# A hybrid attention block: softmax rows left unnormalised, inverse sums carried through DRAM into the gate factor, and three orders changed

## The chip, the core and the metric

The kernel runs on one core of one Trainium2 chip. The metric is the device time of one execution in microseconds (us); three runs of the kernel before had a median of 450.83 us (450.81 to 453.52). The engines are TensorE (PE in the profile; PEld is its loading of weights), VectorE (DVE), ScalarE (ACT), GpSimd (POOL) and SyncE (SP), each with one queue of instructions that it works off in order.

## What is computed

The input x is 512 x 1024 float32. A root-mean-square norm and one wide projection give, for two attention branches of 8 heads of 64 each, q, k, v and a gate input z, and for the merge two gate inputs ga and gb. Cut to what matters here:

```
h = rms_norm(x, norm_g);  proj = h @ w_in          # fq fk fv fz mq mk mv mz ga gb fl
p = softmax(logits, axis=-1);  y = p @ v           # per head; fox: forget bias, moba: rope, causal
y_fox  = from_heads(fox_attention(...))  * silu(fz)
y_moba = from_heads(moba_attention(...)) * silu(mz)
merged = sigmoid(ga + b0) * (y_fox @ w_fox) + sigmoid(gb + b1) * (y_moba @ w_moba)
out = x + merged @ w_out
```

Each row of p is exp(logit - max) over its sum. The row of p is a query's, so the same number divides the whole output row of that query and head; the gate factor silu(z) multiplies that output row element by element.

## The kernel before

**Precision.** Products are float32 made of three matmuls: each operand is split into a rounded part (hi, written by ACT) and the rest (lo, by DVE), and hi*hi, hi*lo and lo*hi are summed in PSUM. `split` (L107) does it for weights: ACT copies (L110), and DVE subtracts (L112). With its argument `half` set, DVE subtracts the first two of four parts (128x512) and POOL the last two, both on L112; without it DVE subtracts all (128x1024). `HALF[0]`, which stands for that argument for projection weights of q, k, v and z, is set at the start of attention.

**Stages.** The program has four. "start" projects the first q and k of the fox branch, norms x, then computes the z units fza and fzb (L372 to L374; the gate factor silu(z) is kept in ZS), the forget bias (`forget`, DVE lines L422 to L447) and the v units fva; between those `make_sums` (L227) builds sums and differences of the normed input's blocks (DVE L236, L240) and stores them in DRAM (POOL L242), for the gates' products. "attention" runs four groups of four heads each: fox a, fox b, moba a, moba b. "gates" computes ga and gb by a scheme of seven products instead of eight for each pair of 256 columns (units GA0, GA1, GB0, GB1; PE L664 to L667; `finish` adds the bias and the sigmoid, L674), reading the sums back (`load_sums`, POOL L249). "end" is the projection by w_moba's rest and w_out.

**One group of attention** (`attn_group`) has pairs of heads. Tr (L475, L477) transposes q and k of a pair; ACT and DVE write QS, KH, KL (L484 to L489). Aa(h) makes a head's logits in four row blocks of 128, 256, 384 and 512 columns (lg, L511, L512); DVE adds the mask and finds the maximum (L514), ACT takes the exponential and, with it, the row sums rs (L516), DVE inverts the sums (L520) and scales the rows of p (L522):

```
if i % 2:
    V.reciprocal(ri[:, hh, i - 1:i + 1], rs[:, hh, i - 1:i + 1])
    for n in range(i - 1, i + 1):
        V.tensor_scalar(pts[n], pts[n], ri[:, hh, n:n + 1], None, op0=OP.mult)
```

Bb(h) transposes p into p_a, p_b and p_cc (L533), splits them (pth by ACT L538, ptl by DVE L539) and multiplies by v (pv, L542, L543); the result, feature by query, is put into ypair by ACT (ysh, L567) and DVE (L568). Yp multiplies the pair's ypair by the gate factor (L577) and splits it (yhf, ylf and so on, L578, L579). The norm of q and k (`ss`, `ff`, L295 to L303) runs on DVE and POOL.

**Order.** The lists `order` and `plan` give for each group the projection units ("filler") that are woven between its pieces by `inter`; `pump` loads and splits their weights a few units ahead, in `order`'s sequence. A tile scheduler then orders the instructions of each engine by its own estimate of time, so that the program's text isn't the final order. Tiles come from pools with a fixed number of buffers by tag.

Of the kernel before, what the change touches and what calls it, by code (L numbers as in the profile page):

```python
# [29 lines left out]
def fox_moba_kernel(ctx: ExitStack, tc, xT, x, w_in, w_fl, w_fox, w_moba, w_out, cst, rope, out):  # L30
# [18 lines left out]
    def t2(tag, bufs, name, shape=(P, 512), dt=F32):  # L49
        pool = stage["pool"] if tag in ("qs", "pt", "ys") else sb  # L50
        return pool.tile(list(shape), dt, name=name, tag=tag, bufs=bufs)
# [176 lines left out]
    def make_sums(k):  # L228
        def tl(tag, dt=F32):
            return stage["pool"].tile([P, 512], dt, name=f"sum_{tag}", tag=tag, bufs=2)  # L230
        a, b = XT[k], XT[k + 4]
        f0, f1 = tl("sf"), tl("sf")
        s3, s2, s1, s4 = f0[:, 0:HT], f0[:, HT:S], f1[:, 0:HT], f1[:, HT:S]
        for o, x, y, op in ((s3, a[:, 0:HT], a[:, HT:S], OP.subtract), (s1, a[:, HT:S], b[:, HT:S], OP.add),
                            (s2, s1, a[:, 0:HT], OP.subtract), (s4, b[:, 0:HT], s2, OP.subtract)):
            V.tensor_tensor(out=o, in0=x, in1=y, op=op)  # L236
        for i, f in enumerate((f0, f1)):
            hl = [tl("sh", F32R), tl("sl", F32R)]
            A.activation(hl[0], f, AF.Copy)
            V.tensor_tensor(out=hl[1], in0=f, in1=hl[0].bitcast(F32), op=OP.subtract)  # L240
            for d, t in zip(S_dram, hl):
                nc.gpsimd.dma_start(out=d[2 * i:2 * i + 2, :, k, :].rearrange("s p t -> p s t"),  # L242
                                    in_=t.bitcast(F32).rearrange("p (s t) -> p s t", t=HT))
# [155 lines left out]
    def zero_kl():  # L399
        for o in range(2):  # L400
            KLt[o] = [stage["pool"].tile([P, S], F32R, name=f"KL{o}{b}") for b in range(2)]
            Q2t[o] = stage["pool"].tile([P, S], F32R, name=f"Q2{o}")
            rows = slice(HD, P) if o == 0 else slice(0, HD)
            for tl in KLt[o] + [Q2t[o]]:
                G.memset(tl[rows, :].bitcast(F32), 0.0)
# [57 lines left out]
    ri = con.tile([P, 16, 4], F32, name="rinv")  # L463

    def attn_group(br, half, gq, gk):
# [36 lines left out]
        def Aa(h):  # L502
            def go():
# [3 lines left out]
                for i in range(NT):  # L507
# [11 lines left out]
                    if i % 2:  # L519
                        V.reciprocal(ri[:, hh, i - 1:i + 1], rs[:, hh, i - 1:i + 1])  # L520
                        for n in range(i - 1, i + 1):
                            V.tensor_scalar(pts[n], pts[n], ri[:, hh, n:n + 1], None, op0=OP.mult)  # L522
                st[h] = pts
            return go

        def Bb(h):
            def go():
# [7 lines left out]
                def spl(p, n):  # L535
                    hi = t2("pt", 6, "pth", dt=F32R)
                    lo = t2("pt", 6, "ptl", dt=F32R)
                    A.activation(hi[:, :n], p[:, :n], AF.Copy)  # L538
                    V.tensor_tensor(out=lo[:, :n], in0=p[:, :n], in1=hi[:, :n].bitcast(F32), op=OP.subtract)  # L539
                    return hi, lo  # L540
# [30 lines left out]
        def Yp(pr):  # L571
            def go():
# [4 lines left out]
                V.tensor_tensor(out=y, in0=y, in1=ZS[br, gp], op=OP.mult)  # L577
# [39 lines left out]
    PRODUCTS = (("A11", 1), ("S3", 3), ("S2", 1), ("A22", 3), ("S1", 1), ("S4", 1), ("A12", 2))  # L617
    groups = {}

    def group(name):  # L620
# [15 lines left out]
        def prep(n):  # L636

            def go():
                if n == 1:
                    sub(R["11"], R["12"], R["11"])  # L640
                    sub(R["12"], R["22"], R["12"])
                elif n == 2:
                    sub(R["12"], R["22"], R["11"])
                elif n == 3:
                    sub(R["12"], R["21"], R["12"])
                key = ("11", "12", "12", "12", "11", "22", "21")[n]
                B[n] = split(R[key], CW, f"{name}{n}")
            return go
        for key, nm, hf, last in (("11", wa, 0, 4), ("12", wb, 0, 3), ("22", wb, 1, 5), ("21", wa, 1, 6)):
# [3 lines left out]
        def product(n):  # L653
            what, b = PRODUCTS[n]
            if n in (0, 1, 6):
# [3 lines left out]
            for c in range(2):  # L659
                o = p[:, c * HT:(c + 1) * HT]  # L660
                cc = slice(c * P, (c + 1) * P)
                for k in range(4):
                    lh, ll = left(what, k)
                    T.matmul(o, hi[:, k, cc], lh, start=(n in (0, 1, 6) and c == 0 and k == 0), stop=False,  # L664
# [14 lines left out]
        def evac(n):  # L679
# [10 lines left out]
            elif n == 2:  # L690
                keep(2, 1)
            elif n == 3:
                add(st["u"][0], 1, 2, 3)
            elif n == 4:
                add(st["u"][1], 1, 3, 1)
            elif n == 5:
                finish(1)
            else:
                add(st["u"][0], 0, 1, 2)
                finish(0)  # L700
# [69 lines left out]
    def out_o(p, n, t):  # L770
        xr = t2("pt", 6, "xr")[:, :CW]
# [6 lines left out]
    order = ["fqa", "fka", "fza", "fzb", "fva", "fqb", "fkb", "mqa", "fvb", "mka", "mva", "mza", "mqb", "mkb", "mvb", "mzb", "wf0", "wf1", "wf2", "wf3",  # L778
# [60 lines left out]
    seq(["fza", "fzb"])  # L839
    forget()  # L840
    for k, u in enumerate(filler(["fva"])):
        u()
        make_sums(k)
# [3 lines left out]
    plan = (("f", "a", C_FQ, C_FK, ["fqb", "fkb", "mqa", "fvb"]),  # L847
            ("f", "b", C_FQ, C_FK, ["mka", "mva", "mza", "mqb"]),
            ("m", "a", C_MQ, C_MK, ["mkb", "mvb", "mzb"]),
            ("m", "b", C_MQ, C_MK, ["wf0", "wf1", "wf2"]))  # L850
    head, body, tail = attn_group("f", "a", col(C_FQ), col(C_FK))
    HALF[0] = True
    head[0]()
    for n in range(4):
# [8 lines left out]
        inter(body + ([following] if n < 3 else []) + tail, filler(plan[n][4]))  # L863
# [71 lines left out]
```

## Time and profile before

| | |
|---|---|
| median of three runs | 450.83 us (450.81 to 453.52) |
| the profiled execution | 448.01 us, span 446.3 us, granted clock 0.994 |
| PE busy | 430.0 us, 3092 matmuls |
| DVE, ACT, POOL busy | 332.4, 264.6, 116.1 us |
| DMA | 54.27 MB in 21367 packets |

A row of a group in the profile reads: line, engine, operation, tile written <- tiles read, shape, count | busy us, mean ns of one | idle us of the engine just before, and what ended it. In a timeline row stand the start, the duration, and in brackets the idle time before it with its releaser. The stages of the schedule in the profiled execution: start to 77 us, attention to 295, gates to about 392, the rest to the end.

### The profile page before, as it was taken

What the parts mean: (1) busy time and instruction counts of PE and PEld (TensorE: products, weight loads), DVE (VectorE), ACT (ScalarE), POOL (GpSimd) and SP (SyncE); (2) the same over time, 40 slices, a digit from 0 to 9 for tenths busy, and PEclk for the clock granted to TensorE, in tenths of its full rate; (3) what the DMA queues carried; (4) which work ended last, traced back from release to release, by engine and by line L of the source; (5) the groups of instructions that cost most, each with busy time, mean ns of one, the idle gap of its engine ahead of it and who ended that gap; (6) DMA issues with size and microseconds to landing.
All of it is one profiled execution on the core that took longest, in us unless ns stands there. A gap on an engine that the chain in (4) does not pass through costs nothing. (4 is left out here: it accounts for less than half of the span.)

```text
span 446.3 us, 8159 instructions
## 1 busy us (share of the span) xinstructions
PE 430.0 (96%) x3092; PEld 403.3 (90%) x3092; DVE 332.4 (74%) x640; ACT 264.6 (59%) x491; POOL 116.1 (26%) x135
## 2 busy tenths in 40 slices
PE   7999999999989999999999999989999999999996
PEld 6997799899989998899898878879999989989996
DVE  4569997758976897859998789967878795574311
ACT  5776445577665856976685896846646635532100
POOL 4038056940556482237640001110000000000000
PEclk9999999999999999999999999989999999999999
DMA  8971277534304223312303212472052605634321
GB/s 262 368 277 50 86 239 230 171 102 126 110 1 131 74 71 95 106 26 87 100 15 118 67 41 74 127 285 95 18 171 57 227 2 170 210 116 142 95 72 48
DMA packets 21367, 54.27 MB, mean 122 GB/s; under 512 B 2960, under 2 KB 7184, under 8 KB 21328
## 3 DMA queue, kind: packets, MB, share of 16 engines
q1 hardware_dynamic: 14240, 39.98, 27.6%
q0 software_dynamic: 2432, 8.39, 5.0%
q10 hardware_dynamic: 4656, 5.38, 4.6%
q8 instruction: 24, 0.39, 0.4%
q14 instruction: 15, 0.12, 0.1%
HBM read 44.17 MB, written 6.29 MB: 113 GB/s over the span
## 5 line engine op out<-in xcount | busy, mean ns | idle before, releaser
L516 ACT ACTIVATE p<-p,negm 128x128 f32<-128x128 f32 (+1 forms) x64 | 35.7, 558 | 22.5 <-DVE negm L514 22.3
L514 DVE CUSTOM_DVE_ANT_0 p<-lg,mask 128x128 f32<-128x128 f32 (+1 forms) x64 | 30.3, 484 | 7.6 <-PE lg L512 7.1
L301 POOL TENSOR_TENSOR ff<-ss,mh 128x8 f32<-128x8 f32 x16 | 27.8, 1744 | 19.4 <-DVE ss L299 15.9
L522 DVE TENSOR_SCALAR p<-p,rinv 128x128 f32<-128x128 f32 (+1 forms) x64 | 28.2, 483 | 0.8
L764 PE MATMUL po<-wh_wo,mgh 128*128 128x256 f32 x96 | 27.1, 282 | 0.0
L765 PE MATMUL po<-wl_wo,mgh 128*128 128x256 f32 x96 | 26.9, 280 | 0.0
L766 PE MATMUL po<-wh_wo,mgl 128*128 128x256 f32 x96 | 26.9, 280 | 0.0
L774 DVE TENSOR_TENSOR ot<-po,xr 128x256 f32<-128x256 f32 x16 | 6.6, 424 | 24.1 <-PE po L766 21.0
L112 DVE TENSOR_TENSOR wl_GB<-wr_gb,wh_GB 128x1024 fp32r<-128x1024 f32 x14 | 16.9, 1222 | 7.0 <-ACT wh_GB L110 7.0
L110 ACT ACTIVATE wh_GB<-wr_gb 128x1024 fp32r<-128x1024 f32 x14 | 14.5, 1058 | 12.0 <-DVE wr_gb L628 6.1
L112 DVE TENSOR_TENSOR wl_GA<-wr_ga,wh_GA 128x1024 fp32r<-128x1024 f32 x14 | 16.9, 1222 | 5.8 <-ACT wh_GA L110 5.7
L511 PE MATMUL lg<-KH,QS 128*128 128x128 f32 (+1 forms) x64 | 20.7, 330 | 0.4 <-DVE negm L514 0.4
L110 ACT ACTIVATE wh_wo<-wr_wo 128x1024 fp32r<-128x1024 f32 x8 | 8.5, 1062 | 18.0 <-PE po L766 7.9
L765 PEld LDWEIGHTS po<-wl_wo,mgh 128*128 128x128 f32 x96 | 18.1, 189 | 0.0
L766 PEld LDWEIGHTS po<-wh_wo,mgl 128*128 128x128 f32 x96 | 18.1, 189 | 0.0
L764 PEld LDWEIGHTS po<-wh_wo,mgh 128*128 128x128 f32 x96 | 18.1, 188 | 0.0
L110 ACT ACTIVATE wh_GA<-wr_ga 128x1024 fp32r<-128x1024 f32 x14 | 14.5, 1054 | 4.5 <-PE pb_GA L666 3.6
L112 DVE TENSOR_TENSOR wl_wo<-wr_wo,wh_wo 128x1024 fp32r<-128x1024 f32 x8 | 9.8, 1221 | 7.3 <-ACT wh_wo L110 7.3
L484 ACT ACTIVATE QS<-p_qT,cs 64x512 fp32r<-64x512 f32 x16 | 10.8, 678 | 6.0 <-PE lg L511 3.3
L667 PE MATMUL pb_GB<-Gh,wl_GB 128*128 128x256 f32 x48 | 13.6, 283 | 0.5 <-DVE wl_GB L112 0.5
L568 DVE TENSOR_TENSOR ypair<-pv,ysh 64x512 f32<-64x512 f32 x16 | 11.0, 686 | 4.1 <-ACT ysh L567 3.8
L489 DVE SCALAR_TENSOR_TENSOR KL<-p_kT,cs,KH 64x512 fp32r<-64x512 f32 x16 | 12.0, 748 | 2.4 <-ACT KH L487 2.1
(456 smaller groups left out, 1828.7 us busy)
## 6 DMA issues: line engine op xcount, KB each, us to landing
wr_ga<-in_w_in_dram SPq DMA_DIRECT2D x8, 512.0 KB
wr_gb<-in_w_in_dram SPq DMA_DIRECT2D x8, 512.0 KB, 6.0
wr_wo<-in_w_out_dram SPq DMA_DIRECT2D x8, 512.0 KB
xt<-in_xT_dram SPq DMA_DIRECT2D x8, 256.0 KB, 5.0
x<-in_x_dram SPq DMA_DIRECT2D x8, 256.0 KB, 7.7
s_dramh<-sum_sh POOLq DMA_DIRECT2D x8, 256.0 KB, 4.0
s_draml<-sum_sl POOLq DMA_DIRECT2D x8, 256.0 KB, 4.2
KH<-KH ACTq DMA_DIRECT2D x16, 128.0 KB, 2.3
```

What stands on the lines that cost most here:

```text
L110: A.activation(hi[:, :, 0:n], src, AF.Copy)
L112: eng.tensor_tensor(out=lo[:, q, 0:n], in0=src[:, q], in1=hi[:, q, 0:n].bitcast(F32), op=OP.subtract)
L301: G.tensor_tensor(out=f2, in0=ss.rearrange("p t h -> p (t h)"), in1=mh, op=OP.pow)
L489: V.scalar_tensor_tensor(kl[me, :], pk[me, :], gk[me, :], kh[me, :].bitcast(F32), op0=OP.mult, op1=OP.subtract)
L511: T.matmul(lg[:, :n], qs[:, qt], kh[:, :n], start=True, stop=False)
L514: V.tensor_tensor_reduce(pt, lg[:, :n], mask[:, 512 - n:512], -0.125, 3.0e38, op0=OP.add, op1=OP.min, accum_out=mkn[:, hh, i:i + 1])
L516: A.activation(pt, pt, AF.Exp, bias=mkn[:, hh, i:i + 1], scale=-1.0, accum_out=rs[:, hh, i:i + 1])
L522: V.tensor_scalar(pts[n], pts[n], ri[:, hh, n:n + 1], None, op0=OP.mult)
L667: T.matmul(o, lo[:, k, cc], lh, start=False, stop=(k == 3), skip_group_check=True)
L764: T.matmul(p[:, :CW], gh[:, st], hi[:, k, :CW], start=(kk == 0), stop=False)
L765: T.matmul(p[:, :CW], gh[:, st], lo[:, k, :CW], start=False, stop=False)
L766: T.matmul(p[:, :CW], gl[:, st], hi[:, k, :CW], start=False, stop=(kk == KT - 1))
```

## The change

- In Aa the scaling of p's rows is gone; p stays as exponentials. Once per pair of heads `inverse_sums` inverts the pair's sums in one DVE instruction (128x8), stores them to DRAM transposed (r_dram, issued by POOL), and loads them back, for each head as one row of 512 queries spread to 64 partitions (rinv_bc, two loads issued by POOL). In Yp the gate factor is first multiplied into rinv_bc (zr; on POOL, for the last pair on DVE), and ypair is then multiplied by that.
- pth and ptl keep four buffers of 512 and get two of 256 for p_cc; the sums' tiles come from another pool.
- HALF is set to False: weights are split whole, on DVE.
- `forget` is called after the first two z units rather than after all; the `make_sums` calls move from the v units of "start" to the filler of the first group.
- The filler of the groups: fvb ahead of mqa; mqb moves from the second group to the third, mzb from the third to the fourth.
- The seven products of the gates come in another sequence, so that the first half is finished before the last product.
- The memsets of KL and Q2 are issued in another sequence.

In the order of instructions that the scheduler gives for the changed kernel, the sums keep nearly their place; on POOL the 20 weight halves are gone, and 8 stores, 16 loads and 7 products come in.

```
--- before.py
+++ after.py
@@ -47,7 +47,7 @@
         stage["pool"] = stage["guard"].__enter__()
 
     def t2(tag, bufs, name, shape=(P, 512), dt=F32):
-        pool = stage["pool"] if tag in ("qs", "pt", "ys") else sb
+        pool = stage["pool"] if tag in ("qs", "pt", "pc", "ys") else sb
         return pool.tile(list(shape), dt, name=name, tag=tag, bufs=bufs)
 
     def pst(tag, bufs, name):
@@ -227,7 +227,7 @@
 
     def make_sums(k):
         def tl(tag, dt=F32):
-            return stage["pool"].tile([P, 512], dt, name=f"sum_{tag}", tag=tag, bufs=2)
+            return t2("y", 15, f"sum_{tag}", dt=dt)
         a, b = XT[k], XT[k + 4]
         f0, f1 = tl("sf"), tl("sf")
         s3, s2, s1, s4 = f0[:, 0:HT], f0[:, HT:S], f1[:, 0:HT], f1[:, HT:S]
@@ -397,9 +397,13 @@
     KLt, Q2t = {}, {}
 
     def zero_kl():
+
         for o in range(2):
-            KLt[o] = [stage["pool"].tile([P, S], F32R, name=f"KL{o}{b}") for b in range(2)]
             Q2t[o] = stage["pool"].tile([P, S], F32R, name=f"Q2{o}")
+        for b in range(2):
+            for o in range(2):
+                KLt.setdefault(o, []).append(stage["pool"].tile([P, S], F32R, name=f"KL{o}{b}"))
+        for o in range(2):
             rows = slice(HD, P) if o == 0 else slice(0, HD)
             for tl in KLt[o] + [Q2t[o]]:
                 G.memset(tl[rows, :].bitcast(F32), 0.0)
@@ -461,6 +465,7 @@
     mkn = con.tile([P, 16, 4], F32, name="negm")
     rs = con.tile([P, 16, 4], F32, name="rsum")
     ri = con.tile([P, 16, 4], F32, name="rinv")
+    R_dram = dr.tile([16, NT, P], F32, name="r_dram")
 
     def attn_group(br, half, gq, gk):
         fox = br == "f"
@@ -516,12 +521,21 @@
                     A.activation(pt, pt, AF.Exp, bias=mkn[:, hh, i:i + 1], scale=-1.0,
                                  accum_out=rs[:, hh, i:i + 1])
                     pts.append(pt)
-                    if i % 2:
-                        V.reciprocal(ri[:, hh, i - 1:i + 1], rs[:, hh, i - 1:i + 1])
-                        for n in range(i - 1, i + 1):
-                            V.tensor_scalar(pts[n], pts[n], ri[:, hh, n:n + 1], None, op0=OP.mult)
                 st[h] = pts
+                if h % 2:
+                    inverse_sums(h // 2)
             return go
+
+        def inverse_sums(pr):
+
+
+            h0 = hb + 2 * pr
+            V.reciprocal(ri[:, h0:h0 + 2, :], rs[:, h0:h0 + 2, :])
+            rb = st["r", pr] = stage["pool"].tile([P, S], F32, name="rinv_bc", tag="rinv_bc", bufs=1)
+            G.dma_start(out=R_dram[h0:h0 + 2].rearrange("h t p -> p h t"), in_=ri[:, h0:h0 + 2, :])
+            for o in range(2):
+                G.dma_start(out=rb[o * HD:(o + 1) * HD, :],
+                            in_=R_dram[h0 + o].rearrange("t p -> (t p)").partition_broadcast(HD))
 
         def Bb(h):
             def go():
@@ -533,8 +547,9 @@
                     T.transpose(dst, pts[i][:, j * P:(j + 1) * P], ident)
 
                 def spl(p, n):
-                    hi = t2("pt", 6, "pth", dt=F32R)
-                    lo = t2("pt", 6, "ptl", dt=F32R)
+                    tag, w, bufs = ("pt", 512, 4) if n == 512 else ("pc", 256, 2)
+                    hi = t2(tag, bufs, "pth", (P, w), F32R)
+                    lo = t2(tag, bufs, "ptl", (P, w), F32R)
                     A.activation(hi[:, :n], p[:, :n], AF.Copy)
                     V.tensor_tensor(out=lo[:, :n], in0=p[:, :n], in1=hi[:, :n].bitcast(F32), op=OP.subtract)
                     return hi, lo
@@ -574,7 +589,9 @@
                 gp = 2 * (half == "b") + pr
                 yh = t2("y", 15, f"yh{br}{gp}", dt=F32R)
                 yl = t2("y", 15, f"yl{br}{gp}", dt=F32R)
-                V.tensor_tensor(out=y, in0=y, in1=ZS[br, gp], op=OP.mult)
+                zr = st["r", pr]
+                (V if (br, gp) == ("m", 3) else G).tensor_tensor(out=zr, in0=ZS[br, gp], in1=zr, op=OP.mult)
+                V.tensor_tensor(out=y, in0=y, in1=zr, op=OP.mult)
                 A.activation(yh, y, AF.Copy)
                 V.tensor_tensor(out=yl, in0=y, in1=yh.bitcast(F32), op=OP.subtract)
                 Y[br, gp] = (yh, yl)
@@ -614,7 +631,7 @@
 
 
 
-    PRODUCTS = (("A11", 1), ("S3", 3), ("S2", 1), ("A22", 3), ("S1", 1), ("S4", 1), ("A12", 2))
+    PRODUCTS = (("A11", 1), ("S3", 3), ("A12", 2), ("S2", 1), ("S1", 1), ("A22", 3), ("S4", 1))
     groups = {}
 
     def group(name):
@@ -639,20 +656,20 @@
                 if n == 1:
                     sub(R["11"], R["12"], R["11"])
                     sub(R["12"], R["22"], R["12"])
-                elif n == 2:
+                elif n == 3:
                     sub(R["12"], R["22"], R["11"])
-                elif n == 3:
-                    sub(R["12"], R["21"], R["12"])
-                key = ("11", "12", "12", "12", "11", "22", "21")[n]
+                elif n == 5:
+                    sub(R["21"], R["21"], R["12"])
+                key = ("11", "12", "21", "12", "11", "21", "22")[n]
                 B[n] = split(R[key], CW, f"{name}{n}")
             return go
-        for key, nm, hf, last in (("11", wa, 0, 4), ("12", wb, 0, 3), ("22", wb, 1, 5), ("21", wa, 1, 6)):
+        for key, nm, hf, last in (("11", wa, 0, 4), ("12", wb, 0, 5), ("22", wb, 1, 6), ("21", wa, 1, 5)):
             loads.append((load(key, nm, hf), base + last))
         preps.extend(prep(n) for n in range(7))
 
         def product(n):
             what, b = PRODUCTS[n]
-            if n in (0, 1, 6):
+            if n < 3:
                 st[b] = pst(("pj", "tp", "tp")[b - 1], (2, 3, 3)[b - 1], f"pb{b}_{name}")
             p = st[b]
             hi, lo = B[n]
@@ -661,7 +678,7 @@
                 cc = slice(c * P, (c + 1) * P)
                 for k in range(4):
                     lh, ll = left(what, k)
-                    T.matmul(o, hi[:, k, cc], lh, start=(n in (0, 1, 6) and c == 0 and k == 0), stop=False,
+                    T.matmul(o, hi[:, k, cc], lh, start=(n < 3 and c == 0 and k == 0), stop=False,
                              skip_group_check=True)
                     T.matmul(o, hi[:, k, cc], ll, start=False, stop=False, skip_group_check=True)
                     T.matmul(o, lo[:, k, cc], lh, start=False, stop=(k == 3), skip_group_check=True)
@@ -688,16 +705,16 @@
             elif n == 1:
                 keep(3, 3)
             elif n == 2:
+                add(st["u"][0], 0, 1, 2)
+            elif n == 3:
                 keep(2, 1)
-            elif n == 3:
-                add(st["u"][0], 1, 2, 3)
             elif n == 4:
                 add(st["u"][1], 1, 3, 1)
             elif n == 5:
+                add(st["u"][0], 1, 2, 3)
+                finish(0)
+            else:
                 finish(1)
-            else:
-                add(st["u"][0], 0, 1, 2)
-                finish(0)
 
         def finish(q):
             u, j0 = st["u"][q], 2 * i + 4 * q
@@ -768,14 +785,14 @@
         return go
 
     def out_o(p, n, t):
-        xr = t2("pt", 6, "xr")[:, :CW]
+        xr = t2("pt", 4, "xr")[:, :CW]
         nc.sync.dma_start(out=xr, in_=x[t * P:(t + 1) * P, n * CW:(n + 1) * CW])
         o = t2("u", 4, "ot")
         V.tensor_tensor(out=o[:, :CW], in0=p[:, :CW], in1=xr, op=OP.add)
         nc.scalar.dma_start(out=out[t * P:(t + 1) * P, n * CW:(n + 1) * CW], in_=o[:, :CW])
 
 
-    order = ["fqa", "fka", "fza", "fzb", "fva", "fqb", "fkb", "mqa", "fvb", "mka", "mva", "mza", "mqb", "mkb", "mvb", "mzb", "wf0", "wf1", "wf2", "wf3",
+    order = ["fqa", "fka", "fza", "fzb", "fva", "fqb", "fkb", "fvb", "mqa", "mka", "mva", "mza", "mqb", "mkb", "mvb", "mzb", "wf0", "wf1", "wf2", "wf3",
              "GA0", "GA1", "GB0", "wm0", "wm2",
              "GB1", "wm1", "wm3", "wo0", "wo1", "wo2", "wo3"]
     for nm in order[2:]:
@@ -836,20 +853,22 @@
         evac_qk(b2[t], "fka", t)
     normalise()
     pump(0)
-    seq(["fza", "fzb"])
+    fz = filler(["fza", "fzb"])
+    for u in fz[:2]:
+        u()
     forget()
-    for k, u in enumerate(filler(["fva"])):
+    for u in fz[2:]:
         u()
-        make_sums(k)
+    seq(["fva"])
     enter("attention")
     zero_kl()
     rope_tables()
-    plan = (("f", "a", C_FQ, C_FK, ["fqb", "fkb", "mqa", "fvb"]),
-            ("f", "b", C_FQ, C_FK, ["mka", "mva", "mza", "mqb"]),
-            ("m", "a", C_MQ, C_MK, ["mkb", "mvb", "mzb"]),
-            ("m", "b", C_MQ, C_MK, ["wf0", "wf1", "wf2"]))
+    plan = (("f", "a", C_FQ, C_FK, ["fqb", "fkb", "fvb", "mqa"]),
+            ("f", "b", C_FQ, C_FK, ["mka", "mva", "mza"]),
+            ("m", "a", C_MQ, C_MK, ["mqb", "mkb", "mvb"]),
+            ("m", "b", C_MQ, C_MK, ["mzb", "wf0", "wf1", "wf2"]))
     head, body, tail = attn_group("f", "a", col(C_FQ), col(C_FK))
-    HALF[0] = True
+    HALF[0] = False
     head[0]()
     for n in range(4):
         nxt = []
@@ -860,7 +879,14 @@
                 moba_begin()
             nxt.extend(attn_group(br, half, col(cq), col(ck)))
             nxt[0][0]()
-        inter(body + ([following] if n < 3 else []) + tail, filler(plan[n][4]))
+        fill = filler(plan[n][4])
+        if n == 0:
+            for k in range(4):
+                def with_sums(u=fill[2 * k], k=k):
+                    u()
+                    make_sums(k)
+                fill[2 * k] = with_sums
+        inter(body + ([following] if n < 3 else []) + tail, fill)
         if n < 3:
             body, tail = nxt[1:]
     enter("gates")
```

More of the change, by code (lines that the diff above doesn't have):

```diff
@@ L775, in out_o @@
         nc.scalar.dma_start(out=out[t * P:(t + 1) * P, n * CW:(n + 1) * CW], in_=o[:, :CW])
[L778 removed]
+    order = ["fqa", "fka", "fza", "fzb", "fva", "fqb", "fkb", "fvb", "mqa", "mka", "mva", "mza", "mqb", "mkb", "mvb", "mzb", "wf0", "wf1", "wf2", "wf3",
              "GA0", "GA1", "GB0", "wm0", "wm2",
@@ L846, in fox_moba_kernel @@
     rope_tables()
[L847 to L850, printed above, removed]
+    plan = (("f", "a", C_FQ, C_FK, ["fqb", "fkb", "fvb", "mqa"]),
+            ("f", "b", C_FQ, C_FK, ["mka", "mva", "mza"]),
+            ("m", "a", C_MQ, C_MK, ["mqb", "mkb", "mvb"]),
+            ("m", "b", C_MQ, C_MK, ["mzb", "wf0", "wf1", "wf2"]))
     head, body, tail = attn_group("f", "a", col(C_FQ), col(C_FK))
-    HALF[0] = True
+    HALF[0] = False
     head[0]()
```

78 lines of the change are left out of this document (50 added, 28 removed).

## The prediction

> **What bounds the kernel now.** I read the page's head first, then busy time by stretches of the schedule, then TensorE's waits, and last the DVE and POOL rows around the longest of them.
>
> ```profile
> span 446.3 us, 8159 instructions
> PE 430.0 (96%) x3092; PEld 403.3 (90%) x3092; DVE 332.4 (74%) x640; ACT 264.6 (59%) x491; POOL 116.1 (26%) x135
> ```
>
> TensorE (PE) has work in 96% of the span, and the change leaves its 3092 matmuls alone. So no edit can take out more than PE's idle time and its slow time. Where is that? The columns below are the stretch, its length, busy time (and instructions) of PE, PEld, DVE, ACT and POOL, the granted clock, the DMA share and GB/s.
>
> ```profile
> 44.00:77.00 33.00, 31.53 (x216) 28.87 (x217) 30.76 (x71) 16.46 (x27) 12.47 (x15) 1.00 0.56 182
> 77.00:139.00 62.00, 59.47 (x483) 58.07 (x482) 45.97 (x106) 40.11 (x87) 33.79 (x31) 1.00 0.35 104
> 139.00:184.00 45.00, 44.83 (x318) 41.76 (x317) 39.17 (x95) 33.55 (x71) 22.33 (x30) 1.00 0.31 91
> 184.00:230.00 46.00, 44.76 (x350) 43.02 (x350) 38.64 (x92) 33.94 (x74) 21.08 (x24) 1.00 0.23 70
> 230.00:295.00 65.00, 62.66 (x359) 53.56 (x358) 56.49 (x120) 49.71 (x96) 7.36 (x13) 1.00 0.32 103
> 312.00:392.00 80.00, 78.79 (x594) 75.28 (x594) 61.29 (x63) 42.78 (x60) 0.00 (x0) 1.00 0.38 124
> ...
> 294.00:296.00 2.00, 2.00 (x14) 2.00 (x13) 0.82 (x2) 0.59 (x1) 0.00 (x1) 0.62 0.97 381
> 296.00:298.00 2.00, 2.00 (x12) 2.00 (x12) 1.26 (x2) 1.11 (x2) 0.00 (x0) 0.53 0.95 387
> ```
>
> From 44 to 295 us (attention with its filler projections, and the end of the stage before) PE lacks work for 1.47 + 2.53 + 0.17 + 1.24 + 2.34 = 7.75 us, in 312 to 392 (gate products) for 1.21. DVE is over 80% busy in four of these stretches. In 294 to 298 the clock was granted at 0.62 and 0.53: 2 x 0.38 + 2 x 0.47 = 1.7 us of matmul time. Who kept PE waiting (total, times, longest; then the longest wait of all in the timeline, start, length and, in brackets, the idle time before it):
>
> ```profile
> PE pz_fzb L372 <- DVE fg L422: 1.7, 1, 1.7
> ...
> PE pj_fvb L273 <- DVE v_fvb L311: 1.2, 1, 1.2
> PE p_kT L477 <- DVE QS L485: 1.2, 1, 1.2
> PE pb_GB L664 <- ACT e_GB L674: 0.7, 1, 0.7
> ```
>
> ```profile
> 292.48 0.47 PE L542 MATMUL pv<-pth,v_mvb 128*128 128x512 f32 x1 [1.76 <-DVE ypair L568]
> ```
>
> Four of the five name DVE, and the wait of 1.8 us that ends at 292.48 is the one just ahead of the slow clock. DVE's queue is thus the second limit, and it decides while PE decides the rest.
>
> **The change, part by part.**
>
> ```profile
> L522 DVE TENSOR_SCALAR p<-p,rinv 128x128 f32<-128x128 f32 (+1 forms) x64 | 28.2, 483 | 0.8
> L520 DVE RECIPROCAL rinv<-rsum 128x2 f32<-128x2 f32 x32 | 5.2, 161 | 8.0 <-ACT p L516 7.7
> L112 DVE TENSOR_TENSOR wl_GA<-wr_ga,wh_GA 128x1024 fp32r<-128x1024 f32 x14 | 16.9, 1222 | 5.8 <-ACT wh_GA L110 5.7
> L112 DVE TENSOR_TENSOR wl_mqa<-wr_mqa,wh_mqa 128x512 fp32r<-128x512 f32 x2 | 4.4, 2236 | 2.6 <-ACT wh_mqa L110 2.6
> L112 DVE TENSOR_TENSOR wl_mqb<-wr_mqb,wh_mqb 128x512 fp32r<-128x512 f32 x2 | 1.4, 678 | 0.0
> L112 POOL TENSOR_TENSOR wl_mqa<-wr_mqa,wh_mqa 128x512 fp32r<-128x512 f32 x2 | 2.5, 1294 | 0.0
> ```
>
> *Unnormalised rows.* The 64 scalings (28.2 us) leave DVE. The 32 reciprocals of 128x2 (161 ns) become 8 of 128x8, some 1.3 us for 5.2. DVE sheds 32 us; it gets one zr product (0.7).
>
> *Whole weight splits.* HALF off moves 20 halves of 128x512 from POOL to DVE, ten pairs of tiles: 20 DVE instructions grow from 678 to 1222 ns, 20 x 0.54 = +10.9 us by duration. But the halves cost DVE more than that while POOL runs its own:
>
> ```profile
> 82.01 4.39 DVE L112 TENSOR_TENSOR wl_mqa<-wr_mqa,wh_mqa 128x512 fp32r<-128x512 f32 x2 [2.57 <-ACT wh_mqa L110]
> ...
> 87.03 0.74 DVE L485 SCALAR_TENSOR_TENSOR QS<-p_qT,cs,QS 64x512 fp32r<-64x512 f32 x1
> ```
>
> ```profile
> 81.70 1.06 POOL L303 TENSOR_TENSOR qn_fqb<-qn_fqb,ff 128x512 f32<-128x512 f32 x1
> 82.70 2.54 POOL L112 TENSOR_TENSOR wl_mqa<-wr_mqa,wh_mqa 128x512 fp32r<-128x512 f32 x2
> ```
>
> The same form that takes 678 ns alone took 4.39 us for two, ending about a microsecond after POOL's two: DVE stood behind POOL for 3 us, and the first QS (87.03), for which PE's p_kT waits, stood behind that. If POOL's halves block nothing, the edit costs 10.9; if each delays DVE by its own length less the DVE half's (1294 - 678 = 0.6), it costs -1.4. I take +2. The Trainium skill says the same in "SBUF — State Buffer", Who interferes with whom: a DVE instruction with two SBUF inputs contends with a GpSimd instruction that reads SBUF, and the one that came second is blocked whole; the 4.39 us agrees. DVE's net is -32 + 0.7 + 2, about -29 of some 211 us between 44 and 295.
>
> *What PE gets of it.* The waits on ypair (1.8), QS (1.2) and v_fvb (1.2) are of a DVE queue that falls short by less than the 29 us taken out of it. wl_mqa moves behind fvb's work, so the first QS comes about 4 us sooner. The wait on fg (1.7) is met otherwise: forget is now called after two fz units, so two more units of matmuls stand ahead of its result. With the smaller waits I take the whole 7.75; the named rows alone are 5.9. The 1.7 us of slow clock follow the 1.8 us gap and go with it, if no new gap takes its place. The skill's "TensorE: Matmul & The Clock Gate", Why this matters for your kernels, asks for gaps under some 3 us; here 1.76 us of idle PE came before a clock of 0.62, so the trace is the stricter. In the gates, the new product order closes a bank earlier (finish(0) ahead of the last product), worth the 0.7 of e_GB, between 0 and 1.21. Gains: 7.75 + 1.7 + 0.7 = 10.15.
>
> *Fillers.* mqb moves from group 2 to 3, mzb from 3 to 4. The work is the same; where it stands isn't. In the changed order of instructions the last pz_mzb matmul is followed by a stretch with attention matmuls alone: 20 transposes, 46 blocks of 128 columns of lg, 20 of pv. Then pf begins. Its prices:
>
> ```profile
> 284.23 0.34 PE L511 MATMUL lg<-KH,QS 128*128 128x384 f32 x1
> ...
> 284.81 0.39 PE L512 MATMUL lg<-KL,QS 128*128 128x512 f32 x1
> 285.04 0.60 PE L533 MATMUL p_b<-ident,p 128*128 128x128 f32 x4
> 285.47 0.38 PE L533 MATMUL p_cc<-ident,p 128*128 128x128 f32 x2
> ```
>
> ```profile
> L516 ACT ACTIVATE p<-p,negm 128x128 f32<-128x128 f32 (+1 forms) x64 | 35.7, 558 | 22.5 <-DVE negm L514 22.3
> L516 ACT ACTIVATION_READ_ACCUMULATOR p<-p,negm 128x1 f32 x64 | 12.0, 188 | 0.0
> L484 ACT ACTIVATE QS<-p_qT,cs 64x512 fp32r<-64x512 f32 x16 | 10.8, 678 | 6.0 <-PE lg L511 3.3 <-DVE QS L485 2.5
> L538 ACT ACTIVATE pth<-p_a 128x512 fp32r<-128x512 f32 x16 | 9.4, 588 | 1.2 <-PE p_a L533 1.1
> L110 ACT ACTIVATE wh_wf<-wr_wf 128x1024 fp32r<-128x1024 f32 x4 | 4.2, 1058 | 0.6 <-PE pz_mzb L373 0.6
> ```
>
> Four lg matmuls, fourteen blocks, start between 284.23 and 285.04: 0.058 a block. Four transposes take 0.43. PE needs 20 x 0.108 + 66 x 0.058 = 6.0 us. ACT needs, for 46 of a head's 20 blocks at (35.7 + 12.0)/16 = 2.98 us a head, 6.9; four QS and KH 2.7; splits and the copy of pv about 2.1; two wh_wf 2.1: 13.8. Every lg waits for an exp to free its chain, so PE can stand up to 7.8 us. ACT instructions overlap at their ends, exps of lg issued under the filler run ahead, and the wh_wf can slip: down to 0. I take +4, the middle, and +0.5 for a slow clock behind it (0 to 1.7).
>
> *Inverse sums through DRAM.* Per pair of heads POOL issues one store of 128 x 8 values, 4 bytes each since the target is transposed (1024 pieces), then, after its landing, two broadcast loads, then zr (as L303, 1.06). Eight pairs.
>
> ```profile
> 275.40 0.63 POOL L249 DMA_DIRECT2D S0h<-s_dramh  x1 [42.28 <-DVE p L522]
> L242 POOL DMA_DIRECT2D s_dramh<-sum_sh x8 | 6.0, 754 | 19.7 <-ACT sum_sh L239 17.5 <-ACT qn_fqb L280 2.0
> q0 software_dynamic: 2432, 8.39, 5.0%
> KH<-KH ACTq DMA_DIRECT2D x16, 128.0 KB, 2.3
> wr_gb<-in_w_in_dram SPq DMA_DIRECT2D x8, 512.0 KB, 6.0
> L301 POOL TENSOR_TENSOR ff<-ss,mh 128x8 f32<-128x8 f32 x16 | 27.8, 1744 | 19.4 <-DVE ss L299 15.9 <-DVE rinv L520 2.8 <-DVE ss L297 0.6
> ```
>
> No row has 4-byte pieces. Issue: 0.63 to 0.75 for 128 and 256 pieces; between 0.75 if the count is free and 3.0 if in proportion; I take 1.9. Landing: from KH's 2.3, to 2.3 + 1024 x 147 ns / 16 = 11.7, with q0's 5.0% x 16 x 446.3 / 2432 = 147 ns a packet (of far larger pieces); I take 3.5, nearer to KH. With two loads (1.1 to issue, 2.5 to land) and zr (1.06) a trip holds POOL's in-order queue for 10 us, between 7.5 and 19. Eight trips are 80 us; between 77 and 295 POOL is busy 84.6 of 218 now, and 20 halves of 1.3 us or more (26) leave, so its time suffices. What counts is what stands behind a trip, by the new order and the PE spacings above. Behind the second pair of (m,a) stands mkb's norm (1.74 + 1.06, and about 1 for rope): p_kT of (m,b) asks for it 17.9 us after that pair's last lg, and it is ready after about 14 (3 to spare). Behind the last pair's two issues stands S0h's load: a reciprocal and exp (1.2), 1.9, 3.5, 1.1, its own 0.6 and a landing as wr_gb's 6.0 make 14.3, and with S0l 16; GA's S3 product asks for it after 17.9 (2 to spare). On DVE the last zr waits for the trip with the next head's ptl behind it, which pv wants after 14 to 16. So at 10 us all is hidden under filler and gate matmuls: 0. Without that cover a trip would cost its 10. The Trainium skill speaks against it: "DMA: Bandwidth & Descriptors", Specifications, lists 512 B as the least transfer for line rate and read-modify-write below. By that the price goes towards the upper end, which is the third rival.
>
> Sums in the first group, and the earlier KL memsets, keep nearly their places in the order: 0, covered by filler matmuls.
>
> **Sum.** -10.15 + 4 + 0.5 = -5.65. Against the profiled execution, 448.01 (446.3 and 1.7 around it): 442.4. The runs' median was 450.83, 2.8 above that; the same shift gives 445.2. One per cent, about what can be told from no change, is 4.5 us.
>
> **Rivals.**
> - *Full gain*, 440.7: ACT keeps up in the stretch without filler. For: ACT is 49.71 of 65 us busy now and sheds no filler of its own. Chance 0.17.
> - *Gain spent*, 450.2: stretch at 7.8, clock dip 1.7: -10.15 + 9.5 = -0.65. For: the ACT sum above; against: lg issued under the filler. Chance 0.12.
> - *DRAM trip decides* (slower). Queue POOL, place: mkb's norm ahead of group (m,b), and the last pair. At 19 us a trip each comes 9 us late: 9 - 3 = 6 before (m,b), 9 - 2 = 7 at the last, so -5.65 + 13 = +7.35, 458.2. Two places late by more than 2.8 each, some 5.5 us over my 10, make it slower than now. Against: KH's 2.3 us. Chance 0.16.
> - *DVE isn't relieved as it says*, 447.6: POOL's halves weren't what stretched DVE's (+10.9 instead of +2) and QS, behind whole splits, still comes late; the 1.2 and 1.2 stay: -5.65 + 2.4 = -3.25. Against: the timeline rows at 82. Chance 0.10.
>
> Forecast as summed: 0.45, its own range 442 to 449, with 0.38 below 446.3 (-1%). Faster 0.17 + 0.38 = 0.55; same 0.07 + 0.12 + 0.10 = 0.29; slower 0.16. The range, 439.5 to 455, leaves out the far end of the DRAM rival and gains beyond the full one.
>
> **What would show it.** Right: in the new trace DVE busy near 300 us; no wait of PE on QS, fvb or ypair over 0.5; one stretch before pf with ACT over 90% busy and PE idle 3 to 5 us; rinv_bc's two issues 2.5 to 5 us after r_dram's. Wrong: r_dram landing over 8 us with p_kT or S0h late behind it; waits of PE on DVE as before; no idle PE before pf (full gain); or a granted clock below 0.9 after it.

## The result and the profile after

The changed kernel took 473.12 us (median of four runs, 472.64 to 476.4) against 451.22 for the kernel before: ratio 1.0485, 95% interval 1.0434 to 1.0537. The forecast was 445.2; the time lies past the range and on the other side, beyond even the 458 of the rival with the DRAM trip.

The head of the page of the changed kernel, with the granted clock in the 40 slices:

```profile
span 474.7 us, 8105 instructions
...
PE 435.7 (92%) x3092; PEld 408.9 (86%) x3092; DVE 311.9 (66%) x553; ACT 262.0 (55%) x489; POOL 115.6 (24%) x146
...
PEclk9999999998899977999889889997999999999999
```

DVE shed 20.5 us of busy time, but PE now has 39.0 us of the span without work (16.3 before), and the clock has several dips where it had one. Who kept PE waiting (total, times, longest):

```profile
PE p_kT L482 <- POOL qn_mka L339: 8.1, 1, 8.1
PE p_qT L480 <- POOL qn_mqb L339: 5.6, 1, 5.6
PE pv L558 <- DVE ptl L554: 4.9, 1, 4.9
PE p_kT L482 <- POOL qn_mkb L339: 4.6, 1, 4.6
PE p_kT L482 <- POOL qn_fkb L303: 4.5, 1, 4.5
PE pz_fzb L372 <- DVE fg L426: 2.3, 1, 2.3
```

The waits on QS, v_fvb and ypair of before are gone. In their place stand five of 4.5 to 8.1 us, 27.7 together, and four of them name POOL, each at the last step of a norm (L303) or of rope (L339). POOL is busy 24% of the span, so it isn't short of time. What was it doing? Its timeline ahead of the longest wait (start, length, and in brackets the idle time before with its releaser):

```profile
152.36 1.04 POOL L303 TENSOR_TENSOR qn_mka<-qn_mka,ff 128x512 f32<-128x512 f32 x1
153.35 0.97 POOL L535 DMA_DIRECT2D r_dram<-rinv  x1
...
164.10 1.09 POOL L537 DMA_DIRECT2D rinv_bc<-r_dram  x2 [6.70 <-DMA r_dram<-rinv]
...
171.07 1.26 POOL L593 TENSOR_TENSOR rinv_bc<-zs_fzb,rinv_bc 128x512 f32<-128x512 f32 x1 [5.32 <-DMA rinv_bc<-r_dram]
172.29 1.67 POOL L301 TENSOR_TENSOR ff<-ss,mh 128x8 f32<-128x8 f32 x1
174.04 1.05 POOL L303 TENSOR_TENSOR qn_mka<-qn_mka,ff 128x512 f32<-128x512 f32 x1
...
177.91 0.44 POOL L339 TENSOR_TENSOR qn_mka<-ra,rb 128x128 f32<-128x128 f32 x1
178.30 0.97 POOL L535 DMA_DIRECT2D r_dram<-rinv  x1
```

Between the first norm of mka at 152.4 and the second at 172.3 stands one trip: the store at 153.35, the loads 10.7 us later, zr at 171.07. It holds POOL's queue for 19 us, 12 of them idle, and the second norm of mka stands behind. That norm needs nothing of the trip: DVE had its sums of squares ready at 162.6. PE's p_kT gets it at 178.4. POOL's waits for the store and for the loads, in seven of the eight pairs (total us, times, longest):

```profile
POOL rinv_bc L537 <- DMA r_dram<-rinv: 56.0, 7, 9.2
POOL rinv_bc L593 <- DMA rinv_bc<-r_dram: 30.3, 7, 6.3
```

And the landings (the last number, median us from issue to landing):

```profile
rinv_bc<-r_dram POOLq DMA_DIRECT2D x16, 128.0 KB, 5.3
...
r_dram<-rinv POOLq DMA_DIRECT2D x8, 4.0 KB, 9.5
```

A store of 4 KB lands after 9.5 us; S0h's load of 512 KB in the same trace lands after 4.8. And the waits are paid twice: in the windows around 178 us, PE's work is missing first and slow afterwards (granted clock 0.66 and 0.83, against 1.00 from 150 to 170).

```profile
170.00:180.00 10.00, 1.88 (x11) 1.68 (x10) 4.75 (x7) 2.42 (x4) 8.04 (x9) 0.66 0.17 52
180.00:190.00 10.00, 9.57 (x43) 7.89 (x43) 5.78 (x11) 3.47 (x6) 1.05 (x2) 0.83 0.21 25
```

### The profile page after: what moved, and what is told of

It is laid out like the page before. It is cut to its first block, busy times and chain, and to the rows that moved or that the text cites. A ratio compares the mean times of both kernels' runs of the same rounds, so it can differ in the third digit from the quotient of the medians.

```text
span 474.7 us, 8105 instructions
## 1 busy us (share of the span) xinstructions
PE 435.7 (92%) x3092; PEld 408.9 (86%) x3092; DVE 311.9 (66%) x553; ACT 262.0 (55%) x489; POOL 115.6 (24%) x146
## 2 busy tenths in 40 slices
DMA packets 22390, 56.39 MB, mean 119 GB/s; under 512 B 3472, under 2 KB 7696, under 8 KB 22352
## 4 chain that ended last, share of the span: by engine, by line
PE 58%; DMA 21%; DVE 6%; POOL 6%; ACT 5%; issue 3%; POOLq 0%; DVEq 0%; ACTq 0%
DMA r_dram<-rinv 8%; DMA rinv_bc<-r_dram 6%; PE pb_GB L681 3%; PE pb_GB L684 3%; PE pb_GB L683 3%; PE pb_GA L681 3%; PE pb_GA L684 3%; PE pb_GA L683 3%; PE po L781 2%; PE po L783 2%; PE po L782 2%; POOL ff L301 2%; DMA wr_fka<-in_w_in_dram 2%; DMA x<-in_x_dram 2%; DMA KH<-KH 2%
## 5 line engine op out<-in xcount | busy, mean ns | idle before, releaser
L537 POOL DMA_DIRECT2D rinv_bc<-r_dram x16 | 8.6, 540 | 65.0 <-DMA r_dram<-rinv 56.0
L516 PE MATMUL lg<-KH,QS 128*128 128x128 f32 (+1 forms) x64 | 21.4, 341 | 0.7 <-DMA KH<-KH 0.4
L582 ACT ACTIVATE ysh<-pv 64x512 f32<-64x512 f32 x16 | 9.5, 594 | 18.3 <-PE pv L558 18.1
L492 ACT ACTIVATE KH<-p_kT,cs 64x512 fp32r<-64x512 f32 x16 | 10.8, 678 | 13.0 <-PE p_kT L482 12.8
L535 POOL DMA_DIRECT2D r_dram<-rinv x8 | 7.7, 957 | 38.1 <-DVE negm L519 33.6
```

Of the source, the lines that this page charges most:

```text
L516: T.matmul(lg[:, :n], qs[:, qt], kh[:, :n], start=True, stop=False)
```

## The experiments

Two theories stood against each other. *Trip*: POOL's in-order queue is held by landings of r_dram and rinv_bc, and the norms stand behind it. *Plan*: the norms come late because mqb and mzb were moved and the splits made whole. Each four rows of the table ran on one chip and share their runs of the kernel before (452.42, 448.69 and 451.11 us), so times are best compared within a four.

| kernel | us | ratio to before, 95% |
|---|---|---|
| normalising back | 444.06 | 0.9859, 0.9796 to 0.9922 |
| trip alone | 486.31 | 1.0799, 1.0723 to 1.0874 |
| store of 32 B pieces | 438.09 | 0.9703, 0.9671 to 0.9736 |
| sums spread by PE, no DMA | 442.46 | 0.9798, 0.9757 to 0.9839 |
| sums turned by PE | 455.58 | 1.0135, 1.008 to 1.0191 |
| the same, halves on POOL | 462.85 | 1.0311, 1.0272 to 1.035 |
| the same, filler of before | 455.71 | 1.0184, 1.0124 to 1.0244 |
| trip from SP, zr on DVE | 512.92 | 1.1422, 1.1369 to 1.1476 |
| sums turned by DVE | 438.31 | 0.9730, 0.9697 to 0.9763 |
| the same, with an unread 4 B store | 467.90 | 1.0374, 1.0332 to 1.0415 |
| turned by DVE, filler of before | 443.45 | 0.9838, 0.9803 to 0.9873 |
| turned by DVE, wf0 ahead of mzb | 437.27 | 0.9701, 0.9669 to 0.9734 |

**Normalising back.**

```diff
 # in Aa of the changed kernel; inverse_sums and zr removed
+                    if i % 2:
+                        V.reciprocal(ri[:, hh, i - 1:i + 1], rs[:, hh, i - 1:i + 1])
+                        for n in range(i - 1, i + 1):
+                            V.tensor_scalar(pts[n], pts[n], ri[:, hh, n:n + 1], None, op0=OP.mult)
```

> Changed kernel with the rows of p normalised in Aa as before (64 scalings and 32 reciprocals back on DVE) and no inverse sums through DRAM; the new filler plan, whole weight splits, order of products and buffers stay. Trip theory (POOL's in-order queue is held about 17 us a pair by two landings, and the norms of q and k stand behind it): the five waits of PE of 4.6 to 8.3 us go, DVE gets 32 us back: 448 to 455 us. Plan theory (the norms come late because mqb and mzb were moved and the splits made whole): the waits at the start of the groups stay, 463 us or more.

444.06 us: better than the trip theory's 448. The longest wait of PE on a norm is this one:

```profile
PE p_kT L481 <- POOL qn_mka L339: 0.3, 1, 0.3
```

The rest of the change, without the trip and without the unnormalised rows, is a gain of 1.4% (0.8 to 2.0). The plan theory fell here.

**Trip alone.**

```diff
 # in the kernel before: Aa, inverse_sums, Bb's pt/pc buffers and Yp of the change, nothing else
-                V.tensor_tensor(out=y, in0=y, in1=ZS[br, gp], op=OP.mult)
+                (V if (br, gp) == ("m", 3) else G).tensor_tensor(out=zr, in0=ZS[br, gp], in1=zr, op=OP.mult)
+                V.tensor_tensor(out=y, in0=y, in1=zr, op=OP.mult)
```

> Kernel before with the unnormalised rows and the inverse sums through DRAM alone (and the pt and pc buffers that make room for it); POOL's weight halves, filler plan and product order as before. Trip theory: the same waits on the norms, worse since POOL also has its halves: 468 to 485 us. Plan theory: the norms have their old cover, 446 to 455 us.

486.31 us, 33.9 over its kernel before; in the changed kernel the trip with the unnormalised rows costs 473.12 - 444.06 = 29.1. So the trip costs more beside POOL's halves and the old plan, and a little more than the trip theory's range said. Here the S0h load, behind the last trip in POOL's queue, kept PE waiting longest:

```profile
PE pb_GA L677 <- DMA S0h<-s_dramh: 13.2, 1, 13.2
PE p_kT L478 <- POOL qn_mkb L339: 8.0, 1, 8.0
```

**Store of 32 B pieces.**

```diff
-    R_dram = dr.tile([16, NT, P], F32, name="r_dram")
+    R_dram = dr.tile([8, P, 2, NT], F32, name="r_dram")
-            G.dma_start(out=R_dram[h0:h0 + 2].rearrange("h t p -> p h t"), in_=ri[:, h0:h0 + 2, :])
+            G.dma_start(out=R_dram[h0 // 2], in_=ri[:, h0:h0 + 2, :])
```

> Changed kernel with the store of the inverse sums left untransposed, 128 pieces of 32 B for 1024 pieces of 4 B, and loads of the same size (the factors reach the wrong queries, which costs no time). Piece theory (the number of pieces makes the 9.5 us landing): landing 2.5 to 4.5 us, a trip of 11 us, 455 to 460 us. Round-trip theory (any store to DRAM from POOL takes this long to report): landing 8 us or more, 470 to 476 us.

438.09 us, 35 less, from the shape of a 4 KB store alone. The queue and the bytes are the same, POOL still waits for the landing, and the landing (median us) fell from 9.5:

```profile
rinv_bc<-r_dram POOLq DMA_DIRECT2D x16, 128.0 KB, 3.2
...
r_dram<-rinv POOLq DMA_DIRECT2D x8, 4.0 KB, 1.8
```

So it is the 1024 pieces of 4 B, not DRAM and not POOL's queue as such: 7.7 us for 896 pieces more, about 8.6 ns each, or 137 ns if they are spread evenly over sixteen engines. That isn't one price for every piece: from 8 pieces of 512 B (1.6 us, below) to 128 of 32 B the landing grew by only 0.2 us, 1.7 ns each. At 4 KB more pieces are also smaller pieces, and the runs don't separate the two. The loads behind the store land sooner too (5.3 to 3.2). I had expected a landing of 2.5 to 4.5 and 455 to 460 us: the piece theory had the cause right, and my price for what is left of the trip was too high.

**Sums spread by PE.**

```diff
+            for t in range(NT):
+                G.tensor_copy(zr[:, t * P:(t + 1) * P].rearrange("p (h d) -> p h d", d=HD),
+                              ri[:, h0:h0 + 2, t:t + 1].to_broadcast([P, 2, HD]))
+                T.transpose(rp2[:, t * P:(t + 1) * P], zr[:, t * P:(t + 1) * P], ident)
+            V.tensor_tensor(out=zr, in0=ZS[br, gp], in1=rp2, op=OP.mult)
```

> Changed kernel with the inverse sums turned by PE instead of through DRAM: POOL copies each pair's sums wide (four 128x128 copies), PE makes four transposes a pair, DVE multiplies the gate factor from PSUM; no DMA. Trip theory: no wait on a norm over 1 us, 32 transposes of 0.11 us more: 443 to 449 us. Plan theory: the waits on the norms stay, 462 us or more.

442.46 us, as the trip theory said; no wait on a norm is left. Without any DMA for the sums the change is a gain of 2.0% (1.6 to 2.4).

**Sums turned by PE, then stored as 8 rows of 512 B.**

```diff
+            T.transpose(tr[:8, :P], ri[:, h0:h0 + 2, :].rearrange("p h t -> p (h t)"), ident)
+            V.tensor_copy(rt, tr[:8, :P])
-            G.dma_start(out=R_dram[h0:h0 + 2].rearrange("h t p -> p h t"), in_=ri[:, h0:h0 + 2, :])
+            G.dma_start(out=R_dram[h0:h0 + 2].rearrange("h t p -> (h t) p"), in_=rt)
```

> Changed kernel, but PE turns each pair's 128x8 inverse sums (one transpose of 0.11 us), DVE copies the 8x128 result and POOL stores it as 8 rows of 512 B; loads and zr stay. Piece theory: the landing of the store falls from 9.5 us to about 2, no wait on a norm over 1 us, 437 to 442 us. If it is the round trip to DRAM from POOL's queue at all, and not the pieces: 465 us or more.

455.58 us: neither number. The landing fell to 1.6 us and the norms were in time, but PE's own queue now waited:

```profile
PE p_r L536 <- DVE rinv L533: 5.5, 2, 3.7
PE pz_fzb L372 <- DVE fg L426: 3.5, 1, 3.5
PE pv L561 <- DVE ypair L587: 3.1, 1, 3.1
```

The transpose of the sums stands in PE's order ahead of matmuls that were ready, and waits for a reciprocal that waits for the last exp. It is the same mistake as the trip's, in a dearer queue.

**Halves on POOL** (in the kernel with PE-turned sums).

```diff
-    HALF[0] = False
+    HALF[0] = True
```

> The kernel with PE-turned sums, with the weight halves back on POOL (HALF True). If POOL's halves stretch DVE's as the prediction read it (halves worth about as much DVE time as whole splits, and POOL's queue fuller): 440 to 445 us, 2 to 4 over whole splits. If the halves relieve DVE by their 10.9 us of duration: the same or up to 2 us less than whole splits.

462.85 us, 7.3 above whole splits. DVE's half, 678 ns alone, took 3.1 and 2.8 us on average in two of the ten pairs of tiles:

```profile
L112 DVE TENSOR_TENSOR wl_mqb<-wr_mqb,wh_mqb 128x512 fp32r<-128x512 f32 x2 | 6.1, 3052 | 0.4 <-ACT wh_mqb L110 0.3
L112 DVE TENSOR_TENSOR wl_mva<-wr_mva,wh_mva 128x512 fp32r<-128x512 f32 x2 | 5.6, 2815 | 0.3 <-ACT wh_mva L110 0.3
```

Over the ten pairs the halves took 26.2 us of DVE, where whole splits took 25.3 in the run above: here they relieve DVE of nothing. How much of the 7.3 us came that way is open, since a wait on a norm also came back (qn_mkb, 3.1 us) with POOL busy for 141.4 us, against 109.3.

**Filler of before** (in the kernel with PE-turned sums).

```diff
+    plan = (("f", "a", C_FQ, C_FK, ["fqb", "fkb", "mqa", "fvb"]), ("f", "b", C_FQ, C_FK, ["mka", "mva", "mza", "mqb"]),
+            ("m", "a", C_MQ, C_MK, ["mkb", "mvb", "mzb"]), ("m", "b", C_MQ, C_MK, ["wf0", "wf1", "wf2"]))
```

> The kernel with PE-turned sums, with the filler plan and weight order of before (mqb in group 2, mzb in group 3, mqa ahead of fvb). Prediction's account: the stretch of attention without filler, 4 us of idle PE, moves to the end of group (m,b) and shrinks to the 2 us of before: 436 to 440 us. If the new plan is what keeps the norms in time: waits on qn_mqb or qn_mkb come back, 442 to 448 us.

455.71 us: no difference beside the 455.58. Neither theory's number was met, and no wait on a norm came back. It tells little of the plan, since waits on p_r stood in both (3.6 us here). The question was asked again on a better kernel below.

**Trip from SP, zr on DVE** (4 B pieces kept).

```diff
-            G.dma_start(out=R_dram...)   # and the two loads
+            nc.sync.dma_start(out=R_dram...)
-                (V if (br, gp) == ("m", 3) else G).tensor_tensor(out=zr, in0=ZS[br, gp], in1=zr, op=OP.mult)
+                V.tensor_tensor(out=zr, in0=ZS[br, gp], in1=zr, op=OP.mult)
```

> Changed kernel with its 4-byte store, but the store and the two loads are issued by SP, and all zr products are on DVE, so that POOL's queue waits for neither landing. Queue theory (what stands behind the landing in the issuing queue is what costs): no wait of PE on a norm over 1 us although the landing stays near 9.5 us; weight loads stand on SP instead, 440 to 452 us. Landing theory (the late factor itself delays Yp and what follows): 462 us or more.

512.92 us: the queue theory's number missed, the landing theory's side of it met. No wait on a norm is left, so POOL's queue was indeed what held the norms. But the wait had only moved: to DVE, which stands at zr until the loads land, and to SP. DVE's queue is the dearer one: of PE's waits over 2 us, 50.7 name DVE, 7.7 KH and none a weight that SP loads.

```profile
DVE rinv_bc L593 <- DMA rinv_bc<-r_dram: 82.2, 8, 15.0
```

```profile
SPq L537 <- DMA r_dram<-rinv: 66.7, 7, 10.8
```

**Sums turned by DVE**, stored as 128 pieces of 128 B.

```diff
-    ri = con.tile([P, 16, 4], F32, name="rinv")
+    ri = con.tile([P, 32], F32, name="rinv")      # 8 columns used
+            V.transpose(rt, ri)                    # 32x32 blocks
+            G.dma_start(out=R_dram[h0 // 2].rearrange("c b r -> b c r"), in_=rt)
```

> Changed kernel, but DVE turns each pair's inverse sums in 32x32 blocks (one instruction on 128x32) and POOL stores the result, 128 pieces of 128 B; the loads of whole rows and zr stay, nothing more on PE. Piece theory: landing of the store about 2 us for 9.5, no wait of PE on a norm over 1 us, 437 to 441 us. If the PE-turned kernel was slow because of the trip itself and not because PE's transposes waited for DVE: 450 us or more.

438.31 us: the speed of the 32 B store, with the factors where they belong; the turn takes DVE 209 ns a pair. Its page, its one wait over 2 us and its landing:

```profile
span 436.5 us, 8120 instructions
...
PE 425.6 (98%) x3092; PEld 401.2 (92%) x3092; DVE 309.3 (71%) x562; ACT 261.6 (60%) x489; POOL 113.6 (26%) x146
```

```profile
PE pz_fzb L372 <- DVE fg L426: 2.4, 1, 2.4
```

```profile
r_dram<-rt POOLq DMA_DIRECT2D x8, 16.0 KB, 2.4
```

**An unread store of 4 B pieces beside it.**

```diff
+                if (br, gp) != ("m", 3):
+                    nc.sync.dma_start(out=X_dram[h0 // 2].rearrange("h t p -> p h t"), in_=rs[:, h0:h0 + 2, :])
```

> The kernel with DVE-turned sums, and beside it the old store of 1024 pieces of 4 B a pair (of the sums, seven times, to a place nobody reads), issued by SP, whose queue doesn't wait for its landing. Waiting theory (the 4-byte store costs only because a queue waits for its landing): within 1.5 us of the kernel without it. Contention theory (the pieces hold up the other transfers): 4 us or more above it, with wr or rinv_bc landings longer.

467.90 us, 29.6 more, though nothing waits for that store. The waiting theory, which was mine, fell, and the contention theory's 4 us were far exceeded. Its sign was another one than I had named: the rinv_bc landings stayed at 3.0, but the landing of r_dram, 128 B pieces from POOL's queue, rose from 2.4 to 8.3 us (POOL's waits for it from 11.6 to 49.1 in all), and KH, from ACT's queue, came late:

```profile
PE lg L518 <- DMA KH<-KH: 7.6, 2, 4.0
PE p_kT L484 <- POOL qn_mka L339: 5.9, 1, 5.9
...
r_dram<-rt POOLq DMA_DIRECT2D x8, 16.0 KB, 8.3
```

So a store of such pieces from SP's queue holds up what other queues move. The changed kernel, whose store goes through POOL's queue, shows a sign of the same: from 98 to 110 us, around its first store, the weight queue's (q1) packets took this share of the engines' time (packets, MB, share), first in the changed kernel, then with DVE-turned sums:

```profile
q1 hardware_dynamic: 288, 1.00, 56.7%
```

```profile
q1 hardware_dynamic: 296, 1.03, 25.6%
```

The same bytes took twice the time, 6.8 us of all engines for a megabyte against 3.0. It isn't so around every store: from 178 to 188 us, around the fourth, 0.57 MB took 21.4%, or 3.8 us a megabyte. How much of the changed kernel's loss came through other queues and how much through POOL's own wait wasn't separated: four of its five long waits are behind POOL, the fifth is behind the last zr (ptl), and KH is 0.4 us.

**Filler of before, and wf0 ahead of mzb** (both with DVE-turned sums).

```diff
 # first: order and plan of the kernel before.  second:
-            ("m", "b", C_MQ, C_MK, ["mzb", "wf0", "wf1", "wf2"]))
+            ("m", "b", C_MQ, C_MK, ["wf0", "mzb", "wf1", "wf2"]))   # and in order
```

> The kernel with DVE-turned sums, with the filler plan and weight order of before. By the prediction's account the stretch without filler (4 us of idle PE ahead of pf) goes, and waits of about 2 us come at the end of (m,b): 435 to 440 us. Rival: the new plan is worth its place, since the old one brings back the waits on v_fvb and ypair: 441 to 447 us.

> The kernel with DVE-turned sums, with wf0 ahead of mzb in the filler of the last group and in the order of weights, so that pf matmuls are ready in the stretch without filler. If that stretch lacks filler: idle PE ahead of pf falls from 4 to under 2 us, 434 to 438 us. If ACT alone sets its length: the same as without.

The old filler costs 5.1 us (443.45; the rival's number). Of the rival's two waits ypair came back and v_fvb didn't; S0h, which it hadn't named, is the longest:

```profile
PE pb_GA L684 <- DMA S0h<-s_dramh: 3.4, 1, 3.4
PE pv L560 <- DVE ypair L586: 2.3, 1, 2.3
```

With wf0 first the time is 437.27 (436.89 to 437.54, against 437.96 to 439.24): 1 us less, inside the number for a stretch that lacks filler. But the sign isn't there. The stretch without the edit and with it, in windows of 12 and 15 us (the second has mzb's matmuls as filler in its last 5 us):

```profile
243.00:255.00 12.00, 9.83 (x48) 7.75 (x47) 11.53 (x29) 10.94 (x26) 0.00 (x0) 0.86 0.25 73
```

```profile
235.00:250.00 15.00, 12.36 (x69) 9.72 (x67) 12.51 (x32) 13.27 (x31) 0.00 (x0) 1.00 0.25 70
```

PE lacks work for 2.6 us, where it lacked 2.2, so idle time didn't fall, and the number was met by luck; what is better is the clock, 1.00 for 0.86. ACT is busy in 10.94 of the 12 us and in 13.27 of the 15, DVE in 11.53 and 12.51, so in both windows the two are nearly full. With 437.27 us this is the fastest kernel here.

## Why the prediction was wrong

- **Landing of the store, the term that failed.** I bounded it by 2.3 and 11.7 us and chose 3.5, "nearer to KH". It was 9.5. KH is 128 KB, and ACT's queue moves that much in 80 packets (q10 from 98 to 110 us); what the store shared with the upper bound was the count, 1024. That 147 ns a packet reckoned and 137 ns a piece measured lie so close is luck: the packets of q0 held some 3.4 KB each. The loads took 5.3, not 2.5, and the trip 19 us, not 10: the upper end. The issue alone was cheaper than taken (0.96, not 1.9). So the term that I had put at 0, "all is hidden", is 27.7 us of waits and more. My own sign of being wrong, a landing over 8 us with p_kT late behind it, came true. The rival that the trip decides, at 0.16, had the mechanism that the forecast lacked.
- **Places behind the trip.** I found two, mkb's norm and the last pair, and gave each 2 to 3 us to spare (mkb's rather 3.9 by my own 17.9 and 14). Both were hit, by 4.6 and 4.9 us. Three that I hadn't listed were hit as well, at the starts of the groups: fkb, mka and mqb, 18.2 us together. So even the rival's 19 us a trip gave only 13 of waits and 458.2. S0h, which I had put there, wasn't named as a wait in the changed kernel; ptl behind zr was.
- **Clock.** For that rival I left slow clock out. Between the profiled executions of the changed and the DVE-turned kernel the span differs by 474.7 - 436.5 = 38.2 us: 28.1 of idle PE (39.0 - 10.9) and 10.1 of slower matmuls (435.7 - 425.6 busy).
- **Contention.** I treated the store as late only for those who wait for it. The unread store showed that it can make others late.
- **Page and measurement.** The Trainium skill's "DMA: Bandwidth & Descriptors", Specifications, which spoke against the change, had the sign. A step at its 512 B can't be seen in these landings: 4 KB landed in 1.6 us as pieces of 512 B and in 1.8 as pieces of 32 B; only the 4 B pieces took 9.5.
- **DVE's relief.** I took 29 us off DVE; its busy time fell by 20.5 (332.4 to 311.9). One term was read from one row: the mqa pair at 4.39 us is the slowest of ten. All ten pairs of halves took 21.2 us of DVE before, and 26.1 as whole splits in the changed kernel: +5, not +2, and not the rival's +10.9. The waits on QS and v_fvb that this rival kept are gone.
- **What was right.** Without the 4 B store the span fell by 9.8 us (446.3 to 436.5), against my 5.65. QS, v_fvb, ypair and e_GB are no longer waits. The stretch ahead of pf, with ACT 91% busy, cost 12 - 9.83 = 2.2 of idle and, by the window's mean clock, 9.83 x (1 - 0.86) = 1.4 of slow clock, 3.6 for my 4.5. The wait on fg, which I said would go (1.7), is still there (2.4). Of the 4.4 us by which PE's busy time fell (430.0 to 425.6), 1.7 is the dip at 294 to 298, with 1.4 of the new dip against it; the rest has no cause shown.
- **Worth of the parts.** Normalising back is 0.9859, DVE-turned sums 0.9730, on two chips: unnormalised rows are worth about 1.3%, the rest of the change about 1.4%. What the orders, the whole splits and the buffers each give in that wasn't separated; the product order was not tried by itself.

## What to carry to other kernels

Price a small DMA by the number and size of its pieces, and not by its bytes alone: where the far side scatters single values, turn the tile on chip first (here a 32x32 block transpose of 209 ns on DVE ahead of each store, and 35 us went with it). Ask for every wait that a change adds which queue stands still and list all that stands behind it in each stage, not only at the end; moving the wait to a busier queue made it worse. Where an unknown cost decides the sign, try it in the smallest run before summing: here a choice of 3.5 between 2.3 and 11.7 decided the forecast.

## What the runs showed of the hardware that I had not expected

A 4 KB store in 1024 pieces of 4 B landed about 8 us later than the same bytes in 128 or 8 pieces. Around the first such store of the changed kernel the share of the engines' time that another queue's packets took for a megabyte was 56.7% of 12 us, against 25.6%. In POOL's queue the profile's count of packets doesn't show the pieces: the changed kernel and the one with 32 B pieces have 22390 packets each. In SP's queue it does: with the unread store the same 12 us have 1327 packets of q1 for 1.04 MB, where the kernel without it has 296 for 1.03.

A clock below 1 didn't need one long gap. In the DVE-turned kernel the stretch from 243 to 255 us had a mean granted clock of 0.86 with 2.2 us of idle PE; with wf0 first the stretch from 235 to 250 had 1.00 with 2.6. The longest gap of PE in the first is 0.74 us, in the second 1.2 (235.9 to 237.1).
